# Middle blocks stored whole and loaded whole or by rows, last two rows in column halves: gradient of a cross entropy on one Trainium2 core

## The chip, the core and the metric

The kernel runs on one core of one Trainium2 chip. The metric is the device time of one execution in microseconds (us). The kernel before the change took 1248.44 us, the median of 3 runs (1248.36 to 1248.45).

The engines that matter here are VectorE (DVE) and ScalarE (ACT), which compute, and SyncE (SP), which only issues transfers here. A transfer (DMA) is an instruction on the queue of SP or ACT; its bytes are then moved by 16 DMA engines that the queues share. TensorE (PE) and GpSimd (POOL) work only in the first microseconds.

## What is computed

For each of 8 x 1024 rows of 8192 logits, the softmax of the row less a one-hot vector at the row's label:

```python
batch, seq_len, vocab = 8, 1024, 8192
...
logits_max = np.max(logits, axis=-1, keepdims=True)
exp_logits = np.exp(logits - logits_max)
softmax = exp_logits / np.sum(exp_logits, axis=-1, keepdims=True)
...
one_hot[batch_idx, seq_idx, labels] = 1.0
return (softmax - one_hot).astype(np.float32)
```

268.4 MB are read and as many written; nothing is used twice.

## The kernel before

**Tiling.** The 8192 rows are cut into 32 blocks `b` of 256. A block lies in SBUF as 128 partitions with G = 2 neighbouring rows each, so that the two rows of a partition are 64 KB in one piece in HBM, at both ends of the kernel. A "row" `t` in the code is one of the two for all 128 partitions (t = 2b or 2b + 1, written `t0` and `t1`): 128 x 8192 float32, 4.19 MB; a block is 8.39 MB. The tile `X` has three slots; block b uses slot b mod 3, is computed in place and stored from there. So the load of block b + 3 waits until block b has been stored.

**Work on a row.** `row_max(t)` is a maximum on DVE (negated, into `m`). `exponentials(t)` is exp(x - max) in place on ACT, with the row's sum into `s`. `finish(t)` is two instructions on DVE: a reciprocal of the sum, then one scalar_tensor_tensor that multiplies the row by it and subtracts the one-hot row, which is read as bytes from PSUM (`hot`). This second instruction is called the subtraction below. `mark(t)` makes that one-hot row on ACT with two activations (`away`, then `hot`); there is one such buffer for each of the two rows of a block, so `mark(t + 2)` waits for `finish(t)`.

**The order is written out by hand.** Each engine runs its instructions in the order in which the loop over the blocks writes them, and semaphores tie the engines together through `run` (line 71). Since every instruction goes through `run`, the profile gives line 76 to all of them, and groups are told apart by tiles. Three strings have a letter for each block:

- `LOADS`: "w" loads the block with one DMA (128 packets of 64 KB), "r" with one per row (128 packets of 32 KB each), "s" with two per row, of every second partition each, one issued by SP and one by ACT. All other loads are issued by SP.
- `STORES`: "r" stores each row as soon as it is finished, on ACT. With "w" `store` (line 116) does nothing at the block's first row and issues one DMA for both at the second.
- `ORDER`: if the *next* block has "r", its first maximum (and exp) is put ahead of this block's second subtraction (`ahead`); if not, it comes after it.

The waits of a load (line 103) are those stores of block b - 3 that touch the same rows: a load by rows after stores by rows waits for one store per row, a whole load for both.

In order "r" DVE's sequence around a block is: maximum t1, subtraction t0, maximum of the next block's t0, subtraction t1. On ACT: exp t1, store t0, mark t0 + 2, exp of the next block's t0, store t1, mark t1 + 2. SP has nothing but loads. Before the change all 32 blocks have order "r" and stores by rows; blocks 0 to 2 are loaded in halves, 3, 4 and 29 to 31 by rows, 5 to 28 whole. The last row's subtraction is cut in two column halves, and its store waits for the second. At the end ACT waits until the last three blocks' stores have landed.

Of the kernel before, what the change touches and what calls it, by code (L numbers as in the profile page):

```python
# [7 lines left out]
P = 128  # L8
G = 2
SLOTS = 3  # L10

LOADS = "sssrrwwwwwwwwwwwwwwwwwwwwwwwwrrr"
STORES = "rrrrrrrrrrrrrrrrrrrrrrrrrrrrrrrr"
ORDER = "rrrrrrrrrrrrrrrrrrrrrrrrrrrrrrrr"


@with_exitstack
def kernel(
# [6 lines left out]
    nc = tc.nc  # L25
# [10 lines left out]
    N, V = x_nv.shape  # L36
    T = N // P
# [4 lines left out]
    o_b = o_nv.rearrange("(b p j) v -> b p j v", p=P, j=G)  # L42
# [4 lines left out]
    X = const.tile([P, SLOTS, G, V], fp32)  # L47
# [16 lines left out]
    with tc.tile_critical():  # L64
        sem = tc.alloc_semaphore
        got = [[sem(f"got{i}{q}") for q in range(4)] for i in range(SLOTS)]
        put = [[sem(f"put{i}{q}") for q in range(4)] for i in range(SLOTS)]
# [3 lines left out]
        def run(engine, waits, counter, method, **operands):  # L71

            waits = list(dict.fromkeys(waits))
            for w in waits[:-1]:
                engine.wait_ge(*w)  # L75
            instruction = getattr(engine, method)(**operands)  # L76
            for w in waits[-1:]:
                instruction._wait_ge(*w)
            step = 16 if method == "dma_start" else 1
            instruction.then_inc(counter, step)  # L80
            count[counter.name] = count.get(counter.name, 0) + step
            return counter, count[counter.name]

        every, rows = slice(0, P), slice(0, G)
        one = [slice(j, j + 1) for j in range(G)]
        halves = [slice(i, P, 2) for i in range(2)]
        quarters = [slice(i, P, 4) for i in range(4)]
        PIECES = {
            "r": [(every, js) for js in one],
            "s": [(ps, js) for js in one for ps in halves],  # L90
            "w": [(every, rows)],
            "h": [(ps, rows) for ps in halves],
            "q": [(ps, rows) for ps in quarters],
        }

        def meets(a, b):
            sets = [[set(range(*d.indices(n))) for d, n in zip(p, (P, G))] for p in (a, b)]
            return all(x & y for x, y in zip(*sets))

        loaded, stored = {}, {}  # L100
        maxed, summed, marked, finished, freed = {}, {}, {}, {}, {}

        def load(b):
            loaded[b] = []
            before = stored.get(b - SLOTS, [])
            for q, piece in enumerate(PIECES[LOADS[b]]):
                ps, js = piece
                free = [w for other, w in before if meets(piece, other)]
                queue = nc.scalar if LOADS[b] == "s" and ps == halves[1] else nc.sync
                w = run(  # L110
# [5 lines left out]
        def store(t):  # L116
            b, j = divmod(t, G)
            stored.setdefault(b, [])
            for q, piece in enumerate(PIECES[STORES[b]]):
                ps, js = piece  # L120
                if js.stop != j + 1:
                    continue
                w = run(
                    nc.scalar, [finished[t]], put[b % SLOTS][q], "dma_start",
                    out=o_b[b, ps, js, :], in_=X[ps, b % SLOTS, js, :],
                )
                stored[b].append((piece, w))

        def row(t):
            return X[:, t // G % SLOTS, t % G, :]  # L130
# [4 lines left out]
        def row_max(t):  # L135
            b, j = divmod(t, G)
            arrived = {w[0].name: w for piece, w in loaded[b] if meets(piece, (every, one[j]))}
            maxed[t] = run(
                nc.vector, arrived.values(), dve, "tensor_reduce",
                out=m[:, t : t + 1], in_=row(t), axis=mybir.AxisListType.X, op=Alu.max, negate=True,  # L140
            )

        def exponentials(t):
            w = run(
                nc.scalar, [maxed[t]], act, "activation",
                out=row(t), in_=row(t), func=Act.Exp, bias=m[:, t : t + 1], scale=1.0,
                accum_out=s[:, t : t + 1],
            )
            summed[t] = w

        def mark(t):
            if t >= T:
                return
            w = run(
                nc.scalar, ([made] if t < G else [freed[t - G]]) + ([marked[t - 1]] if t else []), act, "activation",
                out=away[:], in_=count16[:], func=Act.Abs, bias=at(word, t), scale=1.0,
            )
            marked[t] = run(
                nc.scalar, [w], act, "activation",
                out=hot[:, t % G, :], in_=away[:], func=Act.Relu, bias=at(unit, t), scale=at(minus, t),  # L160
            )

        def finish(t, n=1):
            w = run(nc.vector, [summed[t]], dve, "reciprocal", out=r[:, t : t + 1], in_=s[:, t : t + 1])
            bytes_ = hot[:, t % G, :].bitcast(u8)
            for i in range(n):
                c = slice(i * V // n, (i + 1) * V // n)
                last = run(
                    nc.vector, [marked[t], w] if i == 0 else [], dve, "scalar_tensor_tensor",
                    out=row(t)[:, c], in0=row(t)[:, c], scalar=r[:, t : t + 1], in1=bytes_[:, c],  # L170
                    op0=Alu.mult, op1=Alu.subtract,
                )
            finished[t] = freed[t] = last

        w_raw = run(nc.scalar, [], lab_got, "dma_start", out=lab_raw[:], in_=lab_bp)
        for b in range(SLOTS):
            load(b)
        w = run(nc.gpsimd, [], pool, "memset", ap=ident[:], constant=0.0)
        w_ident = run(
            nc.gpsimd, [w], pool, "affine_select",  # L180
            out=ident[:], in_=ident[:], compare_op=Alu.not_equal, fill=1.0,
# [8 lines left out]
        for j in range(G):  # L190
            w = run(
                nc.tensor, [w_ident, w_lab], pe, "transpose",
                out=lab_ps[:, j, :], in_=lab_f[:, j, :], identity=ident[:],
            )
        w = run(nc.vector, [w], dve, "tensor_copy", out=lab[:], in_=lab_ps)
        w = run(
            nc.vector, [w], dve, "tensor_scalar",
            out=part[:], in0=lab[:], scalar1=2, scalar2=None, op0=Alu.arith_shift_right,
        )
        w_word = run(  # L200
            nc.vector, [w], dve, "tensor_scalar",
            out=word[:], in0=part[:], scalar1=-1.0, scalar2=None, op0=Alu.mult,
        )
        w = run(
            nc.vector, [w_word], dve, "tensor_scalar",
            out=lab[:], in0=lab[:], scalar1=3, scalar2=None, op0=Alu.bitwise_and,
        )
        w = run(
            nc.vector, [w], dve, "tensor_copy", out=minus[:], in_=lab[:]
        )  # L210
        powers = [256.0**k for k in range(4)]
        w = run(
            nc.vector, [w], dve, "tensor_scalar",
            out=unit[:], in0=minus[:], scalar1=0.0, scalar2=powers[0], op0=Alu.is_equal, op1=Alu.mult,
        )
        for k in (1, 2, 3):
            w = run(
                nc.vector, [w], dve, "tensor_scalar",
                out=part[:].bitcast(fp32), in0=minus[:], scalar1=float(k),
                scalar2=powers[k], op0=Alu.is_equal, op1=Alu.mult,  # L220
            )
            w = run(
                nc.vector, [w], dve, "tensor_tensor",
                out=unit[:], in0=unit[:], in1=part[:].bitcast(fp32), op=Alu.add,
            )
        made_dve = run(
            nc.vector, [w], dve, "tensor_scalar",
            out=minus[:], in0=unit[:], scalar1=-1.0, scalar2=None, op0=Alu.mult,
# [8 lines left out]
        for b in range(B):  # L237
            t0, t1 = b * G, b * G + 1
            nxt = t1 + 1
            if ORDER[b] == "b":  # L240
                if t0 not in maxed:
                    row_max(t0)
                    exponentials(t0)
                row_max(t1)
                exponentials(t1)
                finish(t0)
                store(t0)
                mark(t0 + G)
                finish(t1)
                store(t1)  # L250
                mark(t1 + G)
                if b + SLOTS < B:
                    load(b + SLOTS)
                continue
            if t0 not in maxed:
                row_max(t0)
                exponentials(t0)
            row_max(t1)
            finish(t0)
            exponentials(t1)  # L260
            store(t0)
            mark(t0 + G)
            ahead = nxt < T and ORDER[b + 1] == "r"
            if ahead:
                row_max(nxt)
            finish(t1, 1 if t1 + 1 < T else 2)
            if ahead:
                exponentials(nxt)
            store(t1)
            mark(t1 + G)  # L270
            if b + SLOTS < B:
                load(b + SLOTS)
# [33 lines left out]
```

## Time and profile before

| | us |
|---|---|
| median of 3 runs | 1248.44 |
| the profiled execution's own time | 1248.19 |
| its span (first to last instruction in the profile) | 1246.4 |
| DVE busy | 1120.1 |
| ACT busy | 722.7 |
| DVE idle before maxima, until a load landed | 105.6 |
| median from issue to landing, whole loads (24) | 33.3 |
| median from issue to landing, stores (64) | 30.2 |

How to read the profile's parts that follow. The page's second part cuts the span into 40 equal slices; a digit is the busy share in tenths, and for DMA it is the mean over the 16 engines. Its third part counts packets: a packet is the contiguous piece that one DMA engine moves at a time, here a partition's 64 KB or 32 KB, and a last small one per engine that tells of the landing. The share of a queue is the time of its packets over 16 engines and the span. The chain of waits is followed back from the last instruction: at each step to what released it. The groups by form give shapes, count, busy time in sum, mean in nanoseconds, and the idle time of the engine just before them with what ended it. The table by stretches gives the busy time of each engine between two times.

### The profile page before, as it was taken

The numbers are of one execution on the slowest core, as the hardware profiler recorded it, in microseconds if no ns is written. First come the engines' busy times: TensorE is split into PE (matmuls) and PEld (weight loads), VectorE is DVE, ScalarE is ACT, GpSimd is POOL, SyncE is SP. The second block draws the span as 40 slices with busy tenths as digits, with TensorE's granted clock in tenths as the row PEclk, the third lists the DMA queues.
The fourth block names the chain that finished last, engine by engine and source line by source line (L and its number), as shares of the span: only waits on it lengthen the run. The fifth ranks groups of instructions, "written<-read, shape, count | busy, mean of one in ns | idle before, by whom it ended". The sixth has DMA issues, their size and how long they took to land.

```text
span 1246.4 us, 805 instructions
## 1 busy us (share of the span) xinstructions
PE 0.4 (0%) x2; PEld 0.3 (0%) x2; DVE 1120.1 (90%) x207; ACT 722.7 (58%) x257; POOL 2.3 (0%) x7
## 2 busy tenths in 40 slices
PE   0000000000000000000000000000000000000000
PEld 0000000000000000000000000000000000000000
DVE  5999997888988889888899889998989988899995
ACT  2866664557555565555655556655556565566662
POOL 0000000000000000000000000000000000000000
DMA  9999999999999999999999999999999999999998
GB/s 401 416 430 435 437 432 446 422 430 434 433 434 444 439 419 446 423 429 437 431 442 436 422 432 431 433 438 449 423 423 437 435 445 428 426 434 434 432 430 385
DMA packets 15125, 536.98 MB, mean 431 GB/s; under 512 B 1776, under 2 KB 1776, under 8 KB 1808
## 3 DMA queue, kind: packets, MB, share of 16 engines
q10 hardware_dynamic: 9744, 281.09, 52.3%
q1 hardware_dynamic: 5376, 255.86, 47.5%
q14 instruction: 5, 0.04, 0.0%
HBM read 268.50 MB, written 268.44 MB: 431 GB/s over the span
## 4 chain that ended last, share of the span: by engine, by line
DMA 59%; DVE 26%; issue 11%; ACT 3%; DVEq 0%; ACTq 0%; SPq 0%
DMA X<-in_logits_dram 33%; DMA out_dram<-X 26%; DVE X L76 15%; DVE m L76 10%; ACT X L76 2%; DVEq L64 0%; DVE r L76 0%; ACT hot L76 0%; ACT away L76 0%; ACTq L76 0%; DVEq L75 0%; ACTq L301 0%; SPq L64 0%
## 5 line engine op out<-in xcount | busy, mean ns | idle before, releaser
L76 ACT ACTIVATE X<-X,m 128x8192 f32<-128x8192 f32 x64 | 455.8, 7122 | 365.3 <-DVE m L76 365.3
L76 DVE TENSOR_REDUCE m<-X 128x1 f32<-128x8192 f32 x64 | 555.6, 8682 | 105.6 <-DMA X<-in_logits_dram 105.6
L76 DVE SCALAR_TENSOR_TENSOR X<-X,r,hot 128x8192 f32<-128x8192 f32 (+1 forms) x65 | 560.0, 8616 | 3.8 <-ACT hot L76 1.6
L76 ACT ACTIVATE away<-count,word 128x2048 bf16<-128x2048 int16 x64 | 128.1, 2001 | 127.0 <-DVE X L76 127.0
L76 ACT ACTIVATE hot<-away,unit,minus 128x2048 int32<-128x2048 bf16 x64 | 131.9, 2062 | 2.1
L76 ACT ACTIVATION_READ_ACCUMULATOR X<-X,m 128x1 f32 x64 | 11.9, 186 | 0.0
L76 DVE RECIPROCAL r<-s 128x1 f32<-128x1 f32 x64 | 9.8, 154 | 0.0
L76 ACT ACT_TABLE_LOAD x1 | 1.3, 1283 | 5.4 <-issue 5.4
L76 DVE CAST lab_f<-lab_raw 32x256 f32<-32x256 int32 x1 | 0.5, 511 | 2.8 <-DMA lab_raw<-in_labels_dram 2.8
L76 POOL IOTA count<- 128x2048 int16 x1 | 1.8, 1823 | 0.0
L76 DVE TENSOR_TENSOR unit<-unit,part 128x64 f32<-128x64 f32 x3 | 0.7, 224 | 0.1
L76 DVE CAST lab<-hot 128x64 int32<-128x64 f32 x1 | 0.2, 225 | 0.5 <-PE hot L76 0.5
L76 DVE TENSOR_SCALAR part<-minus 128x64 f32<-128x64 f32 x3 | 0.6, 195 | 0.1
L76 PE MATMUL hot<-ident,lab_f 32*128 32x32 f32 x2 | 0.4, 299 | 3.3 <-DVE lab_f L76 3.3
L76 PEld LDWEIGHTS hot<-ident,lab_f 32*128 32x128 f32 x2 | 0.3, 193 | 3.3 <-DVE lab_f L76 3.3
L76 DVE TENSOR_SCALAR word<-part 128x64 f32<-128x64 int32 x1 | 0.2, 197 | 0.0
L76 DVE TENSOR_SCALAR part<-lab 128x64 int32<-128x64 int32 x1 | 0.2, 195 | 0.0
L76 DVE TENSOR_SCALAR unit<-minus 128x64 f32<-128x64 f32 x1 | 0.2, 195 | 0.0
L76 DVE TENSOR_SCALAR lab<-lab 128x64 int32<-128x64 int32 x1 | 0.2, 195 | 0.0
L76 DVE CAST minus<-lab 128x64 f32<-128x64 int32 x1 | 0.2, 195 | 0.0
L76 DVE TENSOR_SCALAR minus<-unit 128x64 f32<-128x64 f32 x1 | 0.2, 195 | 0.0
L76 POOL TENSOR_SCALAR_AFFINE_SELECT ident<-ident 32x32 f32<-32x32 f32 x1 | 0.2, 202 | 0.1
(5 smaller groups left out, 0.5 us busy)
## 6 DMA issues: line engine op xcount, KB each, us to landing
out_dram<-X ACTq DMA_DIRECT2D x64, 4096.0 KB, 30.2
X<-in_logits_dram SPq DMA_DIRECT2D x10, 4096.0 KB, 27.7
X<-in_logits_dram SPq DMA_DIRECT2D x6, 2048.0 KB, 32.8
X<-in_logits_dram ACTq DMA_DIRECT2D x6, 2048.0 KB, 37.2
X<-in_logits_dram SPq DMA_DIRECT2D x24, 33.3
lab_raw<-in_labels_dram ACTq DMA_DIRECT2D x1, 64.0 KB, 1.8
```

What stands on the lines that cost most here:

```text
L76: instruction = getattr(engine, method)(**operands)
```

## The change

The three strings change. Blocks 3 to 24 are stored whole. Of blocks 5 to 28, which were all loaded whole, ten still are (6, 9, 12, 15, 18, 21, 24, 26, 27 and 28); the other fourteen are loaded by rows. Blocks 2 to 24 have order "n", which the loop knows only as "not r": the block before such a block does not take its first maximum ahead. From block 25 on the order is "r" again.

Rows 62 and 63, the last two, are both subtracted in column halves, and each half has a store of its own, which waits for that half alone: row 62's two are issued by SP, row 63's by ACT. Their packets are 16 KB. The number of DMAs goes from 111 to 105: 40 loads on SP become 54, 64 stores become 42 on ACT and 2 on SP; six loads and the labels on ACT stay. DVE has one instruction more. The unused letters "h" and "q" go.

```diff
--- before.py
+++ after.py
@@ -9,9 +9,9 @@
 G = 2
 SLOTS = 3
 
-LOADS = "sssrrwwwwwwwwwwwwwwwwwwwwwwwwrrr"
-STORES = "rrrrrrrrrrrrrrrrrrrrrrrrrrrrrrrr"
-ORDER = "rrrrrrrrrrrrrrrrrrrrrrrrrrrrrrrr"
+LOADS = "sssrrrwrrwrrwrrwrrwrrwrrwrwwwrrr"
+STORES = "rrrwwwwwwwwwwwwwwwwwwwwwwrrrrrrr"
+ORDER = "rrnnnnnnnnnnnnnnnnnnnnnnnrrrrrrr"
 
 
 @with_exitstack
@@ -84,20 +84,18 @@
         every, rows = slice(0, P), slice(0, G)
         one = [slice(j, j + 1) for j in range(G)]
         halves = [slice(i, P, 2) for i in range(2)]
-        quarters = [slice(i, P, 4) for i in range(4)]
+        sides = [slice(i * V // 2, (i + 1) * V // 2) for i in range(2)]
         PIECES = {
             "r": [(every, js) for js in one],
             "s": [(ps, js) for js in one for ps in halves],
             "w": [(every, rows)],
-            "h": [(ps, rows) for ps in halves],
-            "q": [(ps, rows) for ps in quarters],
         }
 
         def meets(a, b):
             sets = [[set(range(*d.indices(n))) for d, n in zip(p, (P, G))] for p in (a, b)]
             return all(x & y for x, y in zip(*sets))
 
-        loaded, stored = {}, {}
+        loaded, stored, sides_done = {}, {}, {}
         maxed, summed, marked, finished, freed = {}, {}, {}, {}, {}
 
         def load(b):
@@ -116,6 +114,14 @@
         def store(t):
             b, j = divmod(t, G)
             stored.setdefault(b, [])
+            if t >= T - G:
+                for i, cs in enumerate(sides):
+                    w = run(
+                        nc.sync if t == T - G else nc.scalar, [sides_done[t][i]], put[b % SLOTS][G * j + i],
+                        "dma_start", out=o_b[b, every, one[j], cs], in_=X[every, b % SLOTS, one[j], cs],
+                    )
+                    stored[b].append(((every, one[j]), w))
+                return
             for q, piece in enumerate(PIECES[STORES[b]]):
                 ps, js = piece
                 if js.stop != j + 1:
@@ -160,16 +166,17 @@
                 out=hot[:, t % G, :], in_=away[:], func=Act.Relu, bias=at(unit, t), scale=at(minus, t),
             )
 
-        def finish(t, n=1):
+        def finish(t):
             w = run(nc.vector, [summed[t]], dve, "reciprocal", out=r[:, t : t + 1], in_=s[:, t : t + 1])
             bytes_ = hot[:, t % G, :].bitcast(u8)
-            for i in range(n):
-                c = slice(i * V // n, (i + 1) * V // n)
+            sides_done[t] = []
+            for i, c in enumerate(sides if t >= T - G else [slice(0, V)]):
                 last = run(
                     nc.vector, [marked[t], w] if i == 0 else [], dve, "scalar_tensor_tensor",
                     out=row(t)[:, c], in0=row(t)[:, c], scalar=r[:, t : t + 1], in1=bytes_[:, c],
                     op0=Alu.mult, op1=Alu.subtract,
                 )
+                sides_done[t].append(last)
             finished[t] = freed[t] = last
 
         w_raw = run(nc.scalar, [], lab_got, "dma_start", out=lab_raw[:], in_=lab_bp)
@@ -263,7 +270,7 @@
             ahead = nxt < T and ORDER[b + 1] == "r"
             if ahead:
                 row_max(nxt)
-            finish(t1, 1 if t1 + 1 < T else 2)
+            finish(t1)
             if ahead:
                 exponentials(nxt)
             store(t1)
```

## The prediction

> **What bounds the kernel now.** I read the page first: the DMA line of its slices, its packet counts and the queues.
>
> ```profile
> span 1246.4 us, 805 instructions
> ...
> DMA  9999999999999999999999999999999999999998
> ...
> DMA packets 15125, 536.98 MB, mean 431 GB/s; under 512 B 1776, under 2 KB 1776, under 8 KB 1808
> ...
> q10 hardware_dynamic: 9744, 281.09, 52.3%
> q1 hardware_dynamic: 5376, 255.86, 47.5%
> ```
>
> The two queues together keep the 16 DMA engines busy for 99.8% of the span. q1 is SP's queue (loads), q10 is ACT's (stores, and half of the first loads). So transfers bound the kernel, and the question for every edit is whether it makes an engine pass bytes faster or stand idle less. The table by stretches shows where they stand idle (columns: us, PE, PEld, DVE, ACT and POOL busy with counts, PE clock, DMA share, GB/s).
>
> ```profile
> 400.00:440.00 40.00, 0.00 (x0) 0.00 (x0) 35.99 (x7) 23.63 (x9) 0.00 (x0) 1.00 1.03 444
> 440.00:480.00 40.00, 0.00 (x0) 0.00 (x0) 36.79 (x7) 24.42 (x9) 0.00 (x0) 1.00 0.98 423
> 1160.00:1200.00 40.00, 0.00 (x0) 0.00 (x0) 39.89 (x9) 24.62 (x9) 0.00 (x0) 1.00 1.00 433
> 1200.00:1220.00 20.00, 0.00 (x0) 0.00 (x0) 19.96 (x4) 13.83 (x5) 0.00 (x0) 1.00 1.00 431
> 1220.00:1230.00 10.00, 0.00 (x0) 0.00 (x0) 9.96 (x4) 2.60 (x2) 0.00 (x0) 1.00 0.89 383
> 1230.00:1240.00 10.00, 0.00 (x0) 0.00 (x0) 3.18 (x1) 0.00 (x0) 0.00 (x0) 1.00 1.05 449
> ```
>
> A packet counts where it starts, so neighbours wobble about 1.00 (1.03, 0.98). The middle is full; only 1220 to 1230 is short, by 11% of 10 us = 1.1 us. There DVE is busy throughout (9.96): row 62's store can't be issued before its subtraction ends at 1224.2, and row 61's has run out. The chain of waits in order of time shows the middle:
>
> ```profile
> 405.02 26.21 DMA out_dram<-X
> ...
> 431.24 33.23 DMA X<-in_logits_dram
> ...
> 473.29 8.76 DVE X L76
> 482.07 26.55 DMA out_dram<-X
> ```
>
> This is a loop: a block's second store lands, a load three blocks on follows, then DVE takes that block's first maximum *ahead of* the previous block's last subtraction (473.29), then comes the next store. It turns in 482.07 - 405.02 = 77.05 us for two blocks. Two blocks are 33.55 MB, and at 433 GB/s that is 77.5 us: the loop is as long as the full transfers make it, so loosening it gains nothing where the share is 1.00. The groups by form give DVE's prices:
>
> ```profile
> L76 DVE TENSOR_REDUCE m<-X 128x1 f32<-128x8192 f32 x64 | 555.6, 8682 | 105.6 <-DMA X<-in_logits_dram 105.6
> L76 DVE SCALAR_TENSOR_TENSOR X<-X,r,hot 128x8192 f32<-128x8192 f32 x63 | 551.1, 8748 | 3.8 <-ACT hot L76 1.6
> L76 DVE SCALAR_TENSOR_TENSOR X<-X,r,hot 128x4096 f32<-128x4096 f32 x2 | 8.9, 4476 | 0.0
> ```
>
> One maximum and one subtraction follow each other every 17.45 us in the timeline, so a block takes DVE 34.9 us against 38.8 us of transfers (16.78 MB at 433 GB/s). DVE's 105.6 us of idleness is cover.
>
> **The change part by part.** *Order "n" (blocks 2 to 24).* Same 64 maxima and subtractions; the next block's first maximum is no longer ahead of the last subtraction. Inside a block DVE still has no hole: exp of the first row (7.12 + 0.19 us) lies under the second maximum (8.68), exp of the second under the first subtraction (8.75), and the two marks (2.00 + 2.06) under the next DVE operation. A block's last store is issued up to one maximum (8.7 us) earlier. Cost on the path: 0, covered by DVE's 3.9 us per block; without that cover, DVE work shows one for one.
>
> *Whole stores (blocks 3 to 24).* 44 stores on ACT become 22. A first row that used to leave after its own subtraction now waits for the second, 8.9 us in order "n". On ACT the waiting store has behind it the second row's mark, which needs that same subtraction, and the next block's exp, which needs a maximum that DVE takes after it: nobody loses. On SP the load three blocks on waits for the whole store, and SP's later loads wait behind it. What could be late is the transfer engines' next work. Engines run dry only when everything issued has landed. With DVE in block b that means loads up to b+2 lie in SBUF, that is, DVE is two blocks behind. DVE is the faster one, so this can only come at the start, where it began at 15.9 us. There: block 4's store is issued after 10 maxima and 10 subtractions; the trace has 10 and 9 of them done at 184.3, so 184.3 + 8.9 = 193.2, and the first packet about 1.0 us later (the first load is issued at 0.96 and bytes begin near 2). Until then the engines have loads 0 to 5 and stores 0 to 3, 10 x 8.39 = 83.9 MB, which at 433 GB/s from 2.0 lasts to 195.7. Margin 1.5 us, so 0; the next store comes at 228.1, where another 16.8 MB last to 234.5.
>
> *Packet sizes.* Each DMA has one packet per partition and 16 small ones (24 x 144 + 10 x 144 + 6 x 80 = 5376 on q1, 64 x 144 + 6 x 80 + 48 = 9744 on q10). On q10 8576 packets of 32 KB took 0.523 x 16 x 1246.4 = 10430 us, 1.216 us each. On q1 9473 us less 1664 x 1.216 leaves 2.425 us for each of 3072 packets of 64 KB: 7 ns less than two small ones (1 to 14 by the rounding of the shares). 14 fewer whole loads split 1792 packets, 22 whole stores join 2816: net 1024 x 7 ns / 16 = -0.45 us. No 64 KB store is in the trace; its nearest rows are the 64 KB load (2.425) and two 32 KB stores (2.432). If stores gain nothing: +0.8 us; if they lose 7 ns a pair instead: +2.0; at 14 ns: -0.9. I take the load's, as stores and loads of 32 KB have the same rate (281.09 MB in 52.3%, 255.86 in 47.5%).
>
> *Shares between the queues.* In the stretch 440 to 460, with both queues filled nearly all the time, the DMA view says:
>
> ```profile
> q1 hardware_dynamic: 92, 6.03, 69.7%
> q10 hardware_dynamic: 96, 2.62, 30.4%
> ```
>
> About 2 to 1 for loads of 64 KB against stores of 32 KB. For the 14 blocks whose loads are now in rows against wide stores I price the reverse: a third for loads. A row (4.19 MB) beside a wide store then takes 29 us at 144 GB/s, the second 9.7 us more alone. The bytes per block are the same 38.8 us, so 0 while engines never stand idle; the other end is a rival below. The Trainium skill, "DMA: Bandwidth & Descriptors", section "Queues, rings and completion order", says that a DMA engine takes turns between queues packet by packet; this row agrees (69.7 to 30.4), and by that rule the shares do turn round here.
>
> *Last two rows in halves.* The last row was already subtracted in halves; row 62 now too: 2 x 4.476 - 8.748 = 0.2 us more of DVE. Two stores become four. Row 62's are issued by SP, whose last load was issued at 1173.2 and behind which nothing waits. From row 50 the order is that of before, so row 62's first half is done at 1215.45 + 4.48 = 1219.9, its bytes start near 1220.9; row 61's store runs out near 1222.5 (from 1222 to 1224 the share is 0.68). The hole of 1.1 us closes (0.6 by the mean of 0.89 and 1.05 over 20 us; 1.3 by stretches of 2 us from 1220, which have 1.06, 0.68 and 0.61). The four follow 4.4 us apart and move 4.85 us each, so none leaves a hole. 256 packets split: 256 x 7 ns / 16 = +0.1 us. If load 28 lands later, DVE's end moves with it, but the last half needs only 1233.4 + 1.0 + 4.9 = 1239.3 against transfers ending near 1243.3: 4 us of cover.
>
> *Sum*, against the profiled execution's own 1248.19 (1246.4 + 1.8 around): -1.1 - 0.45 + 0.1 = -1.45, so 1246.7. That execution lies 0.25 below the median 1248.44: **1247.0** against the median.
>
> **The rivals.**
> *The hole stays* (1248.1): row 62's first half comes too late because load 28 landed over 1.6 us later, or the hole is only passed on. For it: the start is 1.6 us before the dry point and no more. Against: transfers that are full until then make load 28 no later.
>
> *All ends at their best* (1245.7): hole 1.3, packets 0.9, and a last packet of 16 KB in place of 32 KB, 0.6: -2.8 + 0.1. Against: the rows sit in the middle of those bounds.
>
> *Dry at whole stores* (slower, 1268): between 193 and 196 only block 4's store stands between the engines and nothing. If it is late, load 6 waits for a landing: about 1.7 us of receipt (last bytes near 1244.7, span to 1246.4) and 1.0 to the first packet, 2.7 us. It decides once DVE is 1.5 us later than worked out, and if it came back at each of the 8 blocks of slot 0 from block 3 to 24: 8 x 2.7 = 21.6 us, less 1.45. Once alone: 1249.7. Against: 3.9 us of waiting per block says DVE catches up from block 6 on.
>
> *Loads starve* (1267): loads at a third land 38.7 us after issue where the chain had 33.3; 5.4 less DVE's 3.9 leaves 1.5 us in 14 blocks, 21 us. Against: it needs idle engines, and while loads are late they are what moves.
>
> *Dear wide stores* (1251.8): a 64 KB store packet that takes 20 ns more than two small ones adds 2816 x 20 / 16 = 3.5 us to the +0.8 above. Against: loads of that size are cheaper, not dearer.
>
> **How the numbers follow.** Forecast 0.58 (its own range 1246.2 to 1248.0, the packets' near ends included), hole stays 0.12, all at their best 0.13, dry 0.10 (half of it the single case), dear wide stores 0.04, starved 0.03. A measurement of this kernel can tell about 0.2% from no change, 2.5 us: faster is below 1245.9, slower above 1250.9. Faster is 0.13; slower 0.05 + 0.04 + 0.03 = 0.12; within it 0.58 + 0.12 + 0.05 = 0.75. The range 1245.3 to 1249.8 leaves out the 0.12 above and some 0.04 below.
>
> **What would show it.** Right: DMA share 1.00 in every stretch from 180 to 1242 with no 0.89 near 1225; the queues' shares turned round beside whole stores; DVE's idle time before maxima still near 105 us; the two queues' packet times 0.5 us less per engine. Wrong: a share under 0.95 near 195 (dry), a 64 KB store packet over 2.43 us, or a hole near 1222.

## The result and the profile after

| | before | after |
|---|---|---|
| median, us (4 runs each, same chip) | 1248.45 | 1303.47 |
| lowest to highest | 1248.36 to 1249.32 | 1298.78 to 1309.53 |
| the profiled execution's own time | 1248.19 | 1307.48 |

The changed kernel is slower: 1.0444 times the time before, interval 1.042 to 1.0467. The forecast was 1247.0 with a range that ended at 1249.8.

The GB/s line of the page of before has one number per slice of 31.2 us:

```profile
GB/s 401 416 430 435 437 432 446 422 430 434 433 434 444 439 419 446 423 429 437 431 442 436 422 432 431 433 438 449 423 423 437 435 445 428 426 434 434 432 430 385
```

From the page of the changed kernel:

```profile
span 1305.7 us, 778 instructions
...
DMA  9999999999999999999999999999999699999999
GB/s 404 418 434 434 434 432 436 426 440 398 351 399 428 410 409 402 398 430 438 396 373 434 430 407 392 415 411 414 401 405 407 245 422 432 432 434 434 434 434 390
DMA packets 14261, 536.98 MB, mean 411 GB/s; under 512 B 1680, under 2 KB 1680, under 8 KB 1712
...
q10 hardware_dynamic: 6576, 276.89, 50.6%
q1 hardware_dynamic: 7680, 260.05, 47.8%
...
L76 DVE TENSOR_REDUCE m<-X 128x1 f32<-128x8192 f32 x64 | 554.3, 8680 | 166.3 <-DMA X<-in_logits_dram 166.3
```

The DMA line is as full as it was, except one slice, yet the GB/s line below it, now one number per slice of 32.6 us, wavers between 351 and 440 from the tenth slice on, mostly near 405, drops to 245 once, and comes back to 432 and more at the end. A transfer engine that counts as busy is not one that passes bytes at its rate. The 59.3 us of added span have two parts. Summed from the trace's packet records, packets took 1283.9 us per engine, against 1244.8 before. So 39.2 us are longer packets, though there are fewer of them and the bytes are the same, and the other 20.1 us are engines without work (21.8 now, 1.7 before). DVE is not the cause: its maxima take what they took (8680 ns), and they wait 60.7 us longer for loads, about the whole difference.

The table by stretches of the changed kernel (columns as in the prediction) says where:

```profile
200.00:300.00 100.00, 0.00 (x0) 0.00 (x0) 84.68 (x16) 56.84 (x19) 0.00 (x0) 1.00 1.01 433
300.00:480.00 180.00, 0.00 (x0) 0.00 (x0) 142.45 (x25) 92.92 (x34) 0.00 (x0) 1.00 0.99 400
480.00:990.00 510.00, 0.00 (x0) 0.00 (x0) 427.11 (x75) 274.72 (x98) 0.00 (x0) 1.00 0.99 409
990.00:1060.00 70.00, 0.00 (x0) 0.00 (x0) 62.82 (x11) 45.11 (x16) 0.00 (x0) 1.00 0.80 333
1060.00:1300.00 240.00, 0.00 (x0) 0.00 (x0) 218.31 (x40) 131.26 (x46) 0.00 (x0) 1.00 1.00 431
```

Against 433 GB/s the three middle stretches lack 180 x (1 - 400/433) = 13.7, 510 x (1 - 409/433) = 28.3 and 70 x (1 - 333/433) = 16.2 us: 58.2 of the 59.3. The first whole stores (200 to 300) still run at the full rate; from 300 on they don't; from 1060, where rows are stored again, the rate is back. Only 990 to 1060 has idle engines in a lump (0.80 of 70 us, 14 us).

The chain of waits has the same loop as before, with longer transfers in it:

```profile
348.09 47.54 DMA out_dram<-X
...
395.64 43.84 DMA X<-in_logits_dram
...
992.01 37.14 DMA out_dram<-X
...
1029.17 35.24 DMA X<-in_logits_dram
```

A store and the load that it releases took 26 and 33 us before. The four lines also explain the lump: the store issued at 992.01 landed only at 1029.15, and the load that needs its slot starts at 1029.17. Until then more and more engines had nothing left: the share is 0.49 from 1010 to 1015 and 0.03 from 1025 to 1030.

The trace's packet records, averaged by size and direction, in us, beside the commonest duration of each kind:

```
            before          after           commonest
load 32 KB  1.227           1.249           1.213
load 64 KB  2.421           2.547           2.418
store 32 KB 1.213           1.213           1.213
store 64 KB none            2.527           2.418
```

Over the commonest values, the changed kernel's packets lose 19.3 us per engine in 64 KB stores, 10.3 in 64 KB loads, 12.6 in 32 KB loads and nothing in 32 KB stores, 42.2 in all; before it was 2.7. Half of the loss lies in packets of loads, which the change made no larger. And it lies unevenly. The records name no engine; joined end to start they give 16 sequences, and by this estimate the loss is some 30 to 56 us from engine to engine, where before it was 1 to 4. Each DMA lands in 16 parts, and what waits for it waits for the last: the first part of the store issued at 992.01 landed at 1012.6, the last at 1029.15. Before, the parts of one DMA landed within 7.0 us of each other; from 300 to 1060 half of them did so within 1.7. Now half need more than 6.4 there, a tenth more than 16 us, and the parts of the load issued at 966.15 lay 39.2 apart. So the slowest engine sets when a slot is free, and the others run out: that is the lump of idle time.

### The profile page after: what moved, and what is told of

Read it like the earlier page. It is cut to its first block, busy times and chain, and to the rows that moved or that the text cites. A ratio compares the mean times of both kernels' runs of the same rounds, so it can differ in the third digit from the quotient of the medians.

```text
span 1305.7 us, 778 instructions
## 1 busy us (share of the span) xinstructions
PE 0.4 (0%) x2; PEld 0.3 (0%) x2; DVE 1119.7 (86%) x208; ACT 722.8 (55%) x257; POOL 2.3 (0%) x7
## 4 chain that ended last, share of the span: by engine, by line
DVE 43%; DMA 38%; issue 10%; another core or an unknown queue 6%; ACT 1%; DVEq 0%; ACTq 0%; SPq 0%
DVE X L76 23%; DMA X<-in_logits_dram 21%; DVE m L76 20%; DMA out_dram<-X 17%; ACT X L76 1%; DVE r L76 0%; DVEq L64 0%; ACT hot L76 0%; ACT away L76 0%; ACTq L76 0%; SPq L76 0%; DVEq L75 0%; ACTq L308 0%; SPq L64 0%
## 5 line engine op out<-in xcount | busy, mean ns | idle before, releaser
L76 DVE TENSOR_REDUCE m<-X 128x1 f32<-128x8192 f32 x64 | 554.3, 8680 | 166.3 <-DMA X<-in_logits_dram 166.3
L76 ACT ACTIVATION_READ_ACCUMULATOR X<-X,m 128x1 f32 x64 | 11.9, 187 | 0.0
```

## The experiments

Each is the changed kernel with the edit shown, unless something else is said. Ratios are against the kernel before on the same chip, whose medians lay between 1248.41 and 1248.80. The four kernels that only transfer (m1 to m4) were executed once each.

### Which part of the change: three kernels that undo one part or two

**The halves alone** (e1_tail_only): the three strings of before.

```diff
-LOADS = "sssrrrwrrwrrwrrwrrwrrwrrwrwwwrrr"
-STORES = "rrrwwwwwwwwwwwwwwwwwwwwwwrrrrrrr"
-ORDER = "rrnnnnnnnnnnnnnnnnnnnnnnnrrrrrrr"
+LOADS = "sssrrwwwwwwwwwwwwwwwwwwwwwwwwrrr"
+STORES = "rrrrrrrrrrrrrrrrrrrrrrrrrrrrrrrr"
+ORDER = "rrrrrrrrrrrrrrrrrrrrrrrrrrrrrrrr"
```

> The changed kernel with all three strings of before, so that only the last two rows in halves are left. Every theory: the hole of 1.1 us near 1224 closes, 1247.3 us against 1248.45, DMA share 1.00 from 1220 to 1240. If the halves themselves cost (16 KB packets, SP's queue): 1248.5 or more.

Measured: 1248.2 us (1247.19 to 1248.91, 11 runs), ratio 0.9999, interval 0.999 to 1.0008. In the table by stretches of this kernel the hole is gone:

```profile
1220.00:1230.00 10.00, 0.00 (x0) 0.00 (x0) 9.96 (x4) 1.91 (x2) 0.00 (x0) 1.00 0.97 416
1230.00:1240.00 10.00, 0.00 (x0) 0.00 (x0) 2.62 (x1) 0.00 (x0) 0.00 (x0) 1.00 1.00 428
```

The share of 0.89 became 0.97. These shares count a packet where it starts; with the packets cut at the bounds, the engines' idle time from 1220 to 1230 was 1.1 us before, as the prediction read it, and is now 0. But the end did not move by 1.1 us: the engines now end unevenly, and from 1242 to 1246 they stand idle for 2.7 us each on average, before for 1.4. The hole was passed on.

**Stores by rows, the rest of the change kept** (e8_stores_rows): order "n", the new mix of loads and the halves stay.

```diff
-STORES = "rrrwwwwwwwwwwwwwwwwwwwwwwrrrrrrr"
+STORES = "rrrrrrrrrrrrrrrrrrrrrrrrrrrrrrrr"
```

> The changed kernel with row stores throughout, each issued after its own subtraction; loads every third whole and order n stay. Width and release theories: 1247 to 1250 us. If the loads by rows or order n are the cause: 1285 or more.

Measured: 1248.88 us (1248.25 to 1249.35, 10 runs), ratio 1.0003, interval 0.9994 to 1.0012. So order "n", loads by rows and halves together cost nothing that can be measured. The loss is in the whole stores.

**Two row stores, both released late** (e5_late_rows): both rows of a middle block are issued after the second subtraction, when the whole store would be, but as two DMAs of 32 KB packets.

```diff
-STORES = "rrrwwwwwwwwwwwwwwwwwwwwwwrrrrrrr"
+STORES = "rrrddddddddddddddddddddddrrrrrrr"
...
-            for q, piece in enumerate(PIECES[STORES[b]]):
+            late = STORES[b] == "d"
+            for q, piece in enumerate(PIECES["r" if late else STORES[b]]):
                 ps, js = piece
-                if js.stop != j + 1:
+                if j + 1 < G if late else js.stop != j + 1:
                     continue
```

> The changed kernel, but a whole store is issued as two row stores one behind the other, both only after the second row's subtraction: the moment of release and the waits stay, the packets are 32 KB. Width theory: 1247 to 1250 us, packets at 1.213 us. Release theory: 1290 to 1305 as in the changed kernel.

Measured: 1251.1 us (1250.55 to 1252.41, 9 runs), ratio 1.0023, interval 1.0013 to 1.0032, a little above the expected 1247 to 1250. This is the run that decides: the same bytes issued at the same moment, and 1.0444 has become 1.0023. The late release costs 1251.1 - 1248.88 = 2.2 us; one hole, 0.85 of 20 us from 960, is enough for it. The whole store in one DMA with packets of 64 KB costs the other 4.2%. One thing besides the packets differs: a load by rows now waits only for its own row's store, in place of the whole block's. In the changed kernel the wait for the whole store left no engine idle as long as the rate held (share 1.01 and 433 GB/s from 200 to 300), but how much of the 20.1 us of idle time hangs on it later was not measured apart. The stretch 300 to 900 of the table, of the kernel before:

```profile
300.00:900.00 600.00, 0.00 (x0) 0.00 (x0) 540.04 (x94) 348.37 (x125) 0.00 (x0) 1.00 1.00 434
```

Of the kernel with late rows:

```profile
300.00:900.00 600.00, 0.00 (x0) 0.00 (x0) 541.53 (x93) 349.60 (x124) 0.00 (x0) 1.00 1.00 433
```

Of the changed kernel:

```profile
300.00:900.00 600.00, 0.00 (x0) 0.00 (x0) 511.36 (x89) 327.62 (x119) 0.00 (x0) 1.00 0.99 407
```

The share is 1.00, 1.00 and 0.99; the last number, GB/s, is what differs.

### Does it need a certain mix of loads or a certain order?

**All loads of before** (e3_loads_whole) and **all loads by rows** (e6_all_rows), both with the whole stores kept:

```diff
-LOADS = "sssrrrwrrwrrwrrwrrwrrwrrwrwwwrrr"
+LOADS = "sssrrwwwwwwwwwwwwwwwwwwwwwwwwrrr"
```

```diff
-LOADS = "sssrrrwrrwrrwrrwrrwrrwrrwrwwwrrr"
+LOADS = "sssrrrrrrrrrrrrrrrrrrrrrrrrrrrrr"
```

> The changed kernel with the loads of before (blocks 5 to 28 whole); stores whole and order n stay. Width theory (64 KB store packets beside loads slow the packets of both queues, whatever the loads are): 1290 to 1305 us, 64 KB store packets near 2.53 us on average. Mixed-width theory (a queue of 32 KB against one of 64 KB in the wrong direction upsets the engines' common step): 1247 to 1252, since both queues now have 64 KB. Release theory (whole stores let go late, so the engines' work comes in lumps): 1285 to 1305.

> The changed kernel with every load of blocks 3 to 28 by rows, so 32 KB loads beside 64 KB stores everywhere. Width theory: 1280 to 1310 us, like the changed kernel. Mixed-width theory: slower than the changed kernel, 1305 or more, as its ten 64 KB loads are gone. If it was the switching between row and whole loads: 1247 to 1255.

Measured: with whole loads 1280.73 us, its four runs from 1270.56 to 1296.82; the ratio without the slowest is 1.0232 (1.0182 to 1.0281), and whether that is more than 2% is unclear. With rows 1304.28 us (1299.05 to 1316.09), ratio 1.0476 (1.0422 to 1.053). The stretch 300 to 900, first with whole loads, then with rows:

```profile
300.00:900.00 600.00, 0.00 (x0) 0.00 (x0) 520.52 (x91) 335.11 (x121) 0.00 (x0) 1.00 0.99 421
```

```profile
300.00:900.00 600.00, 0.00 (x0) 0.00 (x0) 496.06 (x87) 321.47 (x116) 0.00 (x0) 1.00 0.97 407
```

Neither mix escapes. With whole loads the loss looks smaller than the expected 1290 to 1305, and it lies elsewhere: 64 KB stores took 2.436 us on average, not 2.53, and 64 KB loads 2.496. That run also speaks against the mixed widths, as both queues had 64 KB there. With rows, longer packets make up only 22 us per engine of the added time and idle engines 29.

**Loads and order of before** (e7_order_r): whole stores, but the next block's first maximum is again ahead of the second subtraction, and blocks 5 to 28 are loaded whole.

```diff
-LOADS = "sssrrrwrrwrrwrrwrrwrrwrrwrwwwrrr"
+LOADS = "sssrrwwwwwwwwwwwwwwwwwwwwwwwwrrr"
...
-ORDER = "rrnnnnnnnnnnnnnnnnnnnnnnnrrrrrrr"
+ORDER = "rrrrrrrrrrrrrrrrrrrrrrrrrrrrrrrr"
```

> The kernel before with stores whole for blocks 3 to 24 (and the last two rows in halves); loads and order r as before, so a whole store also waits behind the next block's first maximum. Width theory: 1270 to 1300 us with slow packets. If order n is needed for the loss: 1247 to 1252.

Measured: 1331.86 us, ratio 1.0668 (1.0652 to 1.0684), more than the expected 1270 to 1300. The same stretch of this kernel:

```profile
300.00:900.00 600.00, 0.00 (x0) 0.00 (x0) 494.04 (x85) 318.33 (x114) 0.00 (x0) 1.00 0.95 393
```

Here the share itself is 0.95: for each of the 22 whole stores the engines stand idle for about 2 us each, 1.3 of them all at once; in all it is 45.9 us per engine. That is the prediction's rival "dry at whole stores", in the order that the change left. Order "n" avoids most of it: with the same loads and stores e3_loads_whole has 11.9 us of idle time. The longer packets are here too, 41.8 us per engine, and in this kernel all in 64 KB loads: those under way when a wide store begins take 3.2 to 4.1 us, not 2.42, and the first ones after the dry moment about 3.1. In between, wide loads and wide stores pass side by side at 2.418 us each. So width beside loads does not slow every packet.

### The width by itself: transfers without computation

**m1_streams**: a kernel that only transfers and leaves out all computation. In each of four stages SP loads 8 blocks into two slots in turn and ACT stores 8 blocks from a third slot, each queue with two blocks under way and no dependency between them.

```diff
+STAGES = [("ws", "wa"), ("rs", "wa"), ("ws", "ra"), ("rs", "ra")]
...
+                        dma(
+                            engines[on], f"got{i % 2}{q}", last.get(("l", i - 2), []),
+                            out=X[:, i % 2, js, :], in_=x_b[ib % 32, :, js, :],
+                        )
...
+                        dma(
+                            engines[on], f"put{i % 2}{q}", last.get(("s", i - 2), []),
+                            out=o_b[ob, :, js, :], in_=X[:, 2, js, :],
+                        )
```

("w" is a packet of 64 KB, "r" of 32 KB; the second letter is the queue, SP or ACT; loads first, then stores.)

> No computation at all: block 0 is loaded once and its copy stored 32 times, so the output is copies of block 0, while other blocks are loaded into two slots and not used. Four stages of 8 loads on SP and 8 stores on ACT, each queue two blocks deep, with a common wait between stages: 64 KB loads beside 64 KB stores, 32 KB loads beside 64 KB stores, 64 KB loads beside 32 KB stores, 32 KB beside 32 KB. Width theory (64 KB store packets beside loads are slow by themselves): the first two stages at 390 to 420 GB/s with packets up to 1.3 times the nominal 1.213 and 2.418 us, the last two at 433. Release theory (it is the waits between compute and transfers that put the engines out of step): all four stages at 433 with nominal packets. Mixed-width theory: only the second stage is slow.

The table by stretches, one from each stage (columns: us, POOL busy, PE clock, DMA share, GB/s):

```profile
60.00:400.00 340.00, 0.00 (x0) 1.00 0.95 343
460.00:700.00 240.00, 0.00 (x0) 1.00 1.00 347
820.00:1000.00 180.00, 0.00 (x0) 1.00 1.00 435
1120.00:1400.00 280.00, 0.00 (x0) 1.00 1.00 433
```

Stores of 64 KB beside loads of either size: 343 and 347 GB/s, below even the expected 390 to 420. Stores of 32 KB beside either: 435 and 433. In the first stage the mean load packet takes 1.26 times the commonest value and the store packet 1.13 times; in the second 1.17 and 1.28. Nothing of the kernel's order, waits or arithmetic is in this.

**m2_streams**: six stages of the same kind. 64 KB stores alone; 64 KB loads alone; both on SP's queue in turn; 32 KB loads alone; 32 KB stores alone; 64 KB loads on ACT and 64 KB stores on SP.

```diff
+STAGES = [("", "wa"), ("ws", ""), ("ws", "ws"), ("rs", ""), ("", "ra"), ("wa", "ws")]
```

> No computation, output copies of block 0 as in the run before. Six stages of 8 blocks: 64 KB stores alone; 64 KB loads alone; 64 KB loads and stores in turn on SP's one queue; 32 KB loads alone; 32 KB stores alone; 64 KB loads on ACT beside 64 KB stores on SP. If wide stores are slow by themselves, the first stage is under 425 GB/s. If they are slow only when some engines read while others write, the four stages alone run at 433, the one queue at 433 too (all engines go through it in the same order), and the last like the first stage of the run before. If the queue that issues matters, the last differs from it.

```profile
40.00:160.00 120.00, 0.00 (x0) 1.00 1.01 437
190.00:330.00 140.00, 0.00 (x0) 1.00 1.00 434
360.00:620.00 260.00, 0.00 (x0) 1.00 1.00 431
...
990.00:1270.00 280.00, 0.00 (x0) 1.00 1.00 434
```

A 64 KB store alone is as fast as a 64 KB load alone: 437 and 434. (Alone, 32 KB loads ran at 433 and 32 KB stores at 424.) The store's price that the prediction took was right for a store that stands alone. One queue for both (431) and exchanged queues (434) also ran at the full rate, which suggested two cures.

### Two cures that failed

**One queue** (e9_one_queue): with the loads of before, the whole stores go on SP, and their blocks' loads are issued one block later, so that nothing waits behind a load that can't start.

```diff
-                    nc.scalar, [finished[t]], put[b % SLOTS][q], "dma_start",
+                    nc.sync if STORES[b] == "w" else nc.scalar, [finished[t]], put[b % SLOTS][q], "dma_start",
...
-            if b + SLOTS < B:
-                load(b + SLOTS)
+            late = [b - 1] if b and STORES[b - 1] == "w" else []
+            for c in late + ([] if STORES[b] == "w" else [b]):
+                if c + SLOTS < B:
+                    load(c + SLOTS)
```

**Its control** (e10_late_loads): the same loads, issued one block later too, but the stores stay on ACT.

> The changed kernel with blocks 5 to 28 loaded whole, and the whole stores issued by SP too, so that wide loads and wide stores go through one queue in one order; each load three blocks on is issued one block later, behind the next store, so that SP doesn't wait with an empty queue. Step theory: 1246 to 1258 us, 64 KB packets at 2.418 us for loads and stores. Width theory (64 KB stores cost by themselves): 1280 or more with packets over 2.5. Release theory (work comes in lumps): packets nominal, but DMA share under 0.97 and 1265 or more.

> As the run before, with the whole stores on ACT's queue again: the same widths and the same late loads, two queues. Step and width theories: 1270 to 1310 us with 64 KB packets over 2.48 us on average. If the late loads and not the one queue did it: the same time as the run before.

Measured: one queue 1289.66 us, ratio 1.0323 (1.0308 to 1.0339); control 1293.59, 1.0363 (1.031 to 1.0415). The intervals overlap, so no gain from one queue is shown in the total. Inside, longer packets add 14.6 us per engine and idle engines 27.2, where the control has 22.6 and 18.0. The stretches of e9_one_queue:

```profile
400.00:900.00 500.00, 0.00 (x0) 0.00 (x0) 445.64 (x78) 286.97 (x101) 0.00 (x0) 1.00 1.00 426
980.00:1010.00 30.00, 0.00 (x0) 0.00 (x0) 20.29 (x4) 10.73 (x5) 0.00 (x0) 1.00 0.29 125
```

426 in the middle, not 433: near each turn between store and load, every 39 us, one packet on most engines takes 2.5 to 3.5 us. And the changeover back to row stores near 985 leaves some 20 us of idle engines. The control, from 300 to 900:

```profile
300.00:900.00 600.00, 0.00 (x0) 0.00 (x0) 517.03 (x89) 332.94 (x119) 0.00 (x0) 1.00 0.99 415
```

**Exchanged queues** (e11_swapped): the edit of e9_one_queue, and in addition the whole loads go on ACT.

```diff
-                queue = nc.scalar if LOADS[b] == "s" and ps == halves[1] else nc.sync
+                queue = nc.scalar if LOADS[b] == "w" or LOADS[b] == "s" and ps == halves[1] else nc.sync
```

> The kernel with whole loads, whole stores and late loads, with the queues exchanged: whole loads of blocks 5 to 28 on ACT, whole stores of blocks 3 to 24 on SP. If the assignment of queues decides: 64 KB packets near 2.42 us, 1247 to 1262. If not: 64 KB packets over 2.48 us and 1275 or more, as with the late loads on two queues before (1293.59).

Measured: 1351.96 us, ratio 1.0829 (1.0811 to 1.0847), the slowest of all. The 64 KB packets are still long (2.505 us for loads, 2.468 for stores; the control has 2.510 and 2.458), and the engines are idle for 81 us, as loads now stand behind ACT's own work: a store lands at 206.82, and the load that it frees is issued only at 222.53, after ACT's marks. In the kernel, exchanging the queues does not shorten the packets.

### What decides in the stream

**m3_kicked**: does it matter how the 16 engines stand to each other when a stage begins? Small extra loads "kick" the engines apart at the start of some stages.

```diff
+STAGES = [
+    (5, "k", "ws", "ra"), (5, "k", "rs", "ra"), (5, "", "wa", "ws"),
+    (5, "k", "wa", "ws"), (6, "", "ws", "wa"), (6, "k", "ws", "ws"),
+]
```

> No computation, output copies of block 0 as in the other streams. Six stages; in those called kicked, four small loads for the first 8, 4, 2 and 1 partitions go ahead on the queue of the loads, so that the 16 engines begin the stage up to 1.5 us apart. Stages: 64 KB loads beside 32 KB stores, kicked; 32 KB beside 32 KB, kicked; 64 KB loads on ACT beside 64 KB stores on SP, not kicked; the same kicked; 64 KB loads on SP beside 64 KB stores on ACT, not kicked; 64 KB loads and stores in turn on SP's one queue, kicked. Step theory (wide stores are slow only while the engines are out of step, some reading while others write): first two at 433 GB/s in spite of the kick, the fourth near 345, the sixth above 420. Third and fifth tell whether the state depends on the queue (345 where SP loads, 434 where ACT does) or on how a stage begins. Width theory without steps: third, fourth and fifth all near 345.

The page's GB/s line, 40 slices of 34.2 us:

```profile
GB/s 351 432 436 442 419 437 353 425 431 438 431 431 350 429 427 431 444 429 356 438 429 429 429 431 318 335 343 343 341 347 343 348 269 404 431 429 429 433 435 368
```

Only the fifth stage (slices 25 to 32: 64 KB loads on SP, 64 KB stores on ACT, without a kick) is slow, at 343. The kicks slowed no other stage; single low slices are the ends of stages. So small kicks of this kind are not what makes transfers slow. The third and fourth stages, with the queues exchanged, ran at 434 and 429; the step theory had asked for 345 in the kicked fourth.

**m4_widths**: stores of 40 + 24, 48 + 16, 56 + 8 and 64 KB per partition beside loads of 64 KB; then 64 KB again, with the loads begun only when the first store has landed; then 32 KB loads on ACT, 64 KB stores on SP; 64 KB loads on ACT, 64 KB stores on SP begun after the first load; 32 KB loads on SP, 64 KB stores on ACT. Four blocks each.

```diff
+STAGES = [
+    ("ws", "40a", ""), ("ws", "48a", ""), ("ws", "56a", ""), ("ws", "64a", ""),
+    ("ws", "64a", "l"), ("ra", "64s", ""), ("wa", "64s", "s"), ("rs", "64a", ""),
+]
```

> No computation, output copies of block 0 as in the other streams. Eight stages of 4 blocks; 64 KB loads on SP unless said otherwise, beside stores on ACT cut into two packets per partition of 40 and 24 KB, of 48 and 16, of 56 and 8, then whole 64 KB; then 64 KB stores whose partner loads begin only when the first store has landed; then, with exchanged queues, 32 KB loads on ACT beside 64 KB stores on SP; 64 KB loads on ACT beside 64 KB stores on SP that begin only when the first load has landed; last 32 KB loads on SP beside 64 KB stores on ACT. If the loss grows with the size: 433, 420, 380, 343 GB/s in the first four; if it takes the full 64 KB: 433 three times, then 343. If the assignment of queues decides: 343 in the fifth, 433 in the sixth and seventh, 345 in the last. If the start decides: 433 in the fifth, under 400 in the seventh.

```profile
40.00:140.00 100.00, 0.00 (x0) 1.00 1.00 419
200.00:300.00 100.00, 0.00 (x0) 1.00 0.99 387
360.00:480.00 120.00, 0.00 (x0) 1.00 0.97 365
560.00:720.00 160.00, 0.00 (x0) 1.00 0.95 347
780.00:860.00 80.00, 0.00 (x0) 1.00 1.00 431
920.00:1000.00 80.00, 0.00 (x0) 1.00 1.00 435
1080.00:1160.00 80.00, 0.00 (x0) 1.00 0.99 426
1260.00:1340.00 80.00, 0.00 (x0) 1.00 1.00 348
```

Two things are in these lines. The loss grows with the width of the widest store packet: 419, 387, 365, 347 GB/s for 40, 48, 56 and 64 KB, where 32 KB gave 435. And the fourth and fifth stages have the same widths, queues and bytes, and differ only in when the loads begin: 347 together with the stores, 431 after the first store has landed. A stream of wide stores beside loads has two regimes, and the start can decide which one holds. It is not all that counts: if the start alone decided, the seventh stage was to stay under 400, and it ran at 426. All five stages with exchanged queues, of m2, m3 and m4, ran at 426 to 435, however they began; every slow one had its loads on SP and its stores on ACT, begun together. The streams do not tell queue and start apart, and in the kernel the exchange was no cure. The changed kernel has both rates too: 433 GB/s in its first stretch of whole stores (200 to 300), 400 to 409 after it.

## Why the prediction was wrong, step by step

- **Packet sizes: wrong, and this is the step that failed.** It priced the 64 KB store, which the trace of before doesn't show, with the words "I take the load's, as stores and loads of 32 KB have the same rate", and bounded the term of -0.45 us by -0.9 and +2.0. The price holds for a store alone (437 GB/s). Beside loads the packet takes 2.527 us on average, not 2.425, and the loads' packets grow too: together packets took 39.2 us more per engine. Both bounds came from rows of packets that do not slow each other, so they could not contain this. The step's second fault was to charge the price to the edited transfers alone; half of it falls on the loads, and unevenly over the engines, which goes with the 20.1 us of idle engines that the sum had at 0. Of the prediction's signs of being wrong, the 64 KB store packet over 2.43 us is the one that came.
- **Dear wide stores** was the right rival in kind, with 0.04 and 1251.8 us: it put 20 ns over two small ones on a packet where 95 were measured (2.527 against 2.432), and nothing on the loads. At 95 ns the stores alone would have given 16.7 us. It was marked down because wide loads are cheap, which says nothing of wide stores beside loads.
- **Whole stores at 0 on the path: nearly right.** The dry point near 195 did not come. The timeline has block 4's store where the sum put it, at 193.2, and the next a little later than 228.1, and with the packets cut at the bounds the engines have no idle time from 180 to 240.

```profile
193.17 0.34 ACTq L76 DMA_DIRECT2D out_dram<-X  x1
...
230.25 0.34 ACTq L76 DMA_DIRECT2D out_dram<-X  x1
```

  The later release by itself cost 2.2 us instead of 0 (late rows against rows). The rival "dry at whole stores" did not happen in this kernel, but it is real: with the order of before the engines are idle for 45.9 us.
- **Order "n" at 0: right.** With the stores by rows, the whole rest of the change is at 1.0003. DVE's 3.9 us of cover per block held.
- **Shares between the queues: right.** From 234 to 262, a whole store beside loads by rows, before the rate fell, the DMA view of the changed kernel has them turned round:

```profile
q10 hardware_dynamic: 138, 8.39, 69.1%
q1 hardware_dynamic: 122, 4.00, 33.0%
```

  "Loads starve" asked for this and for idle engines; the maxima did wait 60.7 us longer for loads, but also where the rate, not the share, was what loads lacked.
- **Last two rows in halves, -1.1 + 0.1: the hole closed, the gain didn't come.** Alone, the edit is at 0.9999. "The hole is only passed on" was the rival "the hole stays", and for this part it was right.

Shown: whole stores with 64 KB packets beside loads are the cause (late rows; streams alone against together), not the later release, order "n", loads by rows or halves. Beside loads, 32 KB stores ran at 432 to 441 GB/s in the middle of every stream and kernel; with 64 KB stores most stretches were slower, but not all. Not shown: what happens inside the engines or the memory that makes both directions slow, what selects the slow regime, and whether the packet's width or the DMA's size counts, as no run stores a block in one DMA with 32 KB packets. No version beat the kernel before; the two nearest (halves alone, stores by rows) can't be told from it.

## What to carry to other kernels

A transfer's price from stretches where it runs alone, or from a row of the other direction, need not hold beside the other direction: before packets are widened on a kernel whose transfers are full, run the two widths against each other on both queues without computation. A DMA share of 0.99 is no sign of health; read GB/s over the same stretch, and the packet time of *every* queue, also of the one that wasn't edited. Release time and packet size are changed together when stores are merged; a variant with the old packets at the new release tells them apart in one run, if what waits for them is kept the same too.

## What the runs showed of the hardware that was not expected

- Two directions can slow each other when the store packets are wide: 64 KB stores beside 64 KB loads moved 343 GB/s (m1_streams), alone either moved 434 to 437, and 32 KB stores beside the same loads 435. The Trainium skill, "DMA: Bandwidth & Descriptors", section "Rules for kernel authors", advises merging small transfers into large ones, at least 1 MiB over 128 partitions for the full rate. The transfers of logits and output here are of 2 to 8 MiB, all but the first loads over 128 partitions, and the kernel with the larger ones was slower; in this range the measurement decides.
- The slow regime can depend on the start: 347 or 431 GB/s with the same transfers (m4_widths). That also fits the changed kernel's own spread, 1298.78 to 1309.53 us, where the kernel before repeats within 1 us; that this is its cause wasn't tried.
- The 16 engines need not stay together: parts of one DMA landed up to 39.2 us apart, 7.0 at most before the change, and its waiters wait for the last.
